# The rounded part of ten convolution weights: a casting transfer from GpSimd in place of ScalarE's copy

## The chip, the cores and the metric

The kernel runs on one core of one Trainium2 chip. The metric is the device time of one execution in microseconds. The engines are named as the profile names them: PE (TensorE), with its weight loads as PEld; DVE (VectorE); ACT (ScalarE); POOL (GpSimd); SP (SyncE, which here only issues transfers). A transfer that SP issues is in the profile's queue "hardware_dynamic", one that GpSimd issues in "software_dynamic".

## What is computed

One layer of a diffusion backbone, for 128 context tokens and 512 latent tokens, with model width 1024. What matters here is the mixer: one input projection feeds grouped-query attention (8 query heads, 2 key heads) and, beside it, a short gated convolution.

```python
h = _rms(x, norm_mix) * (1 + sc1) + sh1
proj = h @ w_in
q, k, v, gb, gc, u = jnp.split(proj, ...)      # 512, 128, 128, 512, 512, 512 columns
attn = _block_attention(rope(rms(q)), concat(ctx_k, rope(rms(k))), concat(ctx_v, v))
y_conv = gb * _short_conv(gc * u, conv_w)      # three taps along the tokens
mix = concat(_rms(attn), _rms(y_conv)) @ w_out
x = x + g1 * mix                               # then a SwiGLU block of width 2816
```

All inputs are float32. The vectors sh1, sc1, g1 and so on come from a separate product with the weights w_ada.

## The kernel before

**Split products.** PE multiplies in a rounded format, float32r. To keep accuracy every operand is kept in two parts: a high part, which is the value rounded to float32r, and a low part, which is the value less the high part. A product is then three matmuls: high by high, high by low and low by high. The helper `split` (line 171) makes the two parts: ScalarE copies into a float32r tile (line 172), VectorE subtracts that from the source (line 173).

**Stages.** Until about 76 us the kernel loads x and the first modulation weights, normalises x, and multiplies for the queries; the order of all engines is written out by hand there (P1SEQ). From there to about 260 us attention and the convolution run together, and here the change lies. PE's order is written by hand in this stage as well (the string SEQ: S is scores, T transposes of the probabilities, O the product with the values, F1 one piece of filler). The order of the other engines in this stage is set by the framework's scheduler from priorities. Then come the output projection and the feed-forward block, again in a hand-written order.

**Filler.** The filler is the convolution's projection (`conv_steps`, line 723) and the rest of the modulation product (`ada_all`, line 770). There are twelve convolution weights of 512 KB, for gc, u and gb in each of four column blocks (the list CONV, line 264). Each is multiplied in two token halves of 320 by eight blocks of 128 rows by three matmuls, at lines 715 to 717. So each weight has 16 matmuls at line 715.

**The weight stream.** Weights come in one list (`plan`, line 208): four for the queries, two for keys and values, the twelve of the convolution with sixteen 1 MB pieces of w_ada between them, and four of w_out. `W(key)` (line 252) is called where PE needs a weight, and loads up to three entries ahead. `load` (line 212) takes a tile wf from a ring of three (WFB) and lets SP load the float32 weight into it. `load_split` (line 233) takes wh and wl from rings of four each (WHB) and calls `split`, with a lowered priority (SOW). A buffer of wh can only be written again when PE has done with the weight four places earlier; a buffer of wf when VectorE's subtraction has read it. SP's queue also carries the small es transfers of attention (lines 909 and 910) and the w_ada pieces; GpSimd's holds the power function of the norms (line 186), four small memsets for each block of the convolution (line 734), and accumulating transfers (lines 755, 921, 922).

The first eight weights of the list, the first two of the convolution among them, are loaded in the first stage and split there by `w_hi` and `w_lo` (lines 532 to 543), which do not pass through `load_split`.

**Attention's chain.** For each head `att_s` (line 844) takes scores from PE (line 850), their maximum on VectorE (856), a scaling on ScalarE (857), the exponent on ScalarE (860), a reciprocal on VectorE (862) and the normalisation on ScalarE or VectorE (864, 866). `att_t` transposes the probabilities on PE (877) and splits them (172 and 173, to ph and pl). `att_o` multiplies by the values (894). The scores have one PSUM tile (tag "s", one buffer), so the next scores wait for the exponent.

Of the kernel before, what the change touches and what calls it, by code (L numbers as in the profile page):

```python
# [12 lines left out]
ALU = mybir.AluOpType  # L13
# [87 lines left out]
SOW = -300  # L101
# [12 lines left out]
def build(ctx, tc, x_prompt, x_sample, cond, cache_k, cache_v, vectors, b_ada, q_norm, k_norm, w_mod, w_ada,  # L114
          w_q, w_kv, w_conv, w_out, w_gate_up, w_down, rope, x_turned, o_turned, o_k, o_v):
    nc = tc.nc
    act, dve, pool, pe, sp = nc.scalar, nc.vector, nc.gpsimd, nc.tensor, nc.sync
# [23 lines left out]
    def T(tag, shape, dt=F32, bufs=1):  # L141
        seq[0] += 1
        return pools[where.get(tag, "A")][1].tile(list(shape), dt, tag=tag, bufs=bufs, name=f"{tag}_{seq[0]}")
# [21 lines left out]
    def f32(ap):  # L165
        return ap.bitcast(F32)

    def early(n):
        return tc.high_priority(n)

    def split(hi, lo, src):
        act.activation(hi, src, AF.Copy)
        dve.tensor_tensor(lo, src, f32(hi), ALU.subtract)
# [38 lines left out]
    def load(e, later=False):  # L212
        key, src, ph, ring, gain, _ = e
        if ring == "op":
            e[5] = [T(x, (P, 8, P), F32R, WHB) for x in ("wh", "wl")]
            with early(SOP[0]):
                split(*e[5], order[place["gu"[key[2] == "A2"], key[1]]][5])
            return
        a, b = src.shape[1], src.shape[2]
        wf = T("aw", (P, a, b), F32, AWB) if ring == "a" else T("wf", (P, a, b), F32, WFB)  # L220
        sp.dma_start(wf, src)
        if ring in "af":
            e[5] = wf
            return
        if later:
            deferred.append((e, wf))
            return
        load_split(e, wf)
# [4 lines left out]
    def load_split(e, wf):  # L233
        key, src, ph, ring, gain, _ = e
        a, b = src.shape[1], src.shape[2]
        wh = T(ring + "h", (P, a, b), F32R, WHB)
        wl = T(ring + "l", (P, a, b), F32R, WHB)
        if gain is None:
            with early(SOW):
                split(wh, wl, wf)  # L240
        else:
            for i in range(a):
                g = vec[:, gain + i:gain + i + 1]
                act.activation(wh[:, i], wf[:, i], AF.Copy, scale=g)
                dve.scalar_tensor_tensor(wl[:, i], wf[:, i], g, f32(wh[:, i]), ALU.mult, ALU.subtract)
        e[5] = (wh, wl)
# [1343 lines left out]
```

## Time and profile before

| What | us |
|---|---|
| Median of 3 runs | 720.96 |
| Lowest and highest run | 719.54, 721.59 |
| The profiled execution, its own time | 720.04 |
| Span of that execution | 718.2 |
| PE busy | 708.6 |
| PE weight loads busy | 678.0 |
| VectorE busy | 539.8 |
| ScalarE busy | 425.1 |
| GpSimd busy | 70.9 |

The span is the time from the first to the last instruction that the profile shows; the execution's own time is 1.84 us longer. A busy time is the sum over an engine's instructions in that one execution. Matmuls overlap in the profile, so PE's idle time is more telling than its busy time. "Idle before" names the work whose end released an instruction, as far as the profile shows it.

### The profile page before, as it was taken

How to read it: one execution, taken by the hardware profiler on the slowest of the kernel's cores; microseconds unless marked ns; L12 is line 12 of the kernel's file. 1: busy time of each engine (PE TensorE's matmuls, PEld its weight loads, DVE VectorE, ACT ScalarE, POOL GpSimd, SP SyncE). 2: the span in 40 equal slices, each digit the busy share in tenths (PEclk: the TensorE clock that was granted, in tenths of full speed). 3: DMA queues.
4: the chain of work that ended last, by engine and by line, in shares of the span. 5: the costliest groups of instructions: out<-in, count | busy, mean ns of one | idle time of the engine just before them, and what ended most of it. 6: DMA issues, size and time to landing. Idle time of an engine off the chain costs nothing.

```text
span 718.2 us, 12650 instructions
## 1 busy us (share of the span) xinstructions
PE 708.6 (99%) x4950; PEld 678.0 (94%) x4950; DVE 539.8 (75%) x976; ACT 425.1 (59%) x801; POOL 70.9 (10%) x101
## 2 busy tenths in 40 slices
PE   8999999999999999999999999999999999999997
PEld 7679798989988999999999999999999999999997
DVE  5767977675766556779988966579789855788895
ACT  6566877676676435565565655556556555465553
POOL 2303201012010121300000011000000011000000
PEclk9999999999999999999999999999999999999999
DMA  8964254546444222831323267522222556322462
GB/s 356 338 217 181 69 188 159 165 155 174 140 117 157 86 76 59 268 109 50 98 65 101 74 151 133 131 81 89 89 89 89 125 129 128 112 67 81 140 207 103
DMA packets 33884, 95.97 MB, mean 134 GB/s; under 512 B 4288, under 2 KB 12608, under 8 KB 31776
## 3 DMA queue, kind: packets, MB, share of 16 engines
q1 hardware_dynamic: 29360, 88.09, 36.2%
q0 software_dynamic: 4176, 7.01, 7.1%
q8 instruction: 39, 0.64, 0.4%
q14 instruction: 21, 0.17, 0.1%
q10 hardware_dynamic: 288, 0.05, 0.0%
HBM read 81.77 MB, written 10.62 MB: 129 GB/s over the span
## 4 chain that ended last, share of the span: by engine, by line
PE 92%; DVE 3%; ACT 3%; DMA 1%; issue 1%; SPq 0%; POOL 0%; DVEq 0%; ACTq 0%; POOLq 0%
PE pf L176 22%; PE pf L177 22%; PE pf L178 22%; PE pc L715 3%; PE pc L716 3%; PE pc L717 3%; PE po L894 3%; PE ps L850 2%; PE pt L877 2%; PE pc L776 2%; PE ps L176 1%; PE ps L178 1%; DMA es<-t 1%; PE ps L177 1%; PE pc L375 1%; PE pc L516 1%
## 5 line engine op out<-in xcount | busy, mean ns | idle before, releaser
L1361 DVE TENSOR_TENSOR wl<-sx,wh 128x1024 fp32r<-128x1024 f32 (+1 forms) x64 | 76.0, 1187 | 45.8 <-ACT wh L1358 45.8
L176 PE MATMUL pf<-B,wh 128*128 128x320 f32 x288 | 88.8, 308 | 0.0
L178 PE MATMUL pf<-B,wl 128*128 128x320 f32 x288 | 88.6, 308 | 0.0
L177 PE MATMUL pf<-B,wh 128*128 128x320 f32 x288 | 88.6, 308 | 0.0
L178 PE MATMUL pf<-T,wl 128*128 128x320 f32 x280 | 86.2, 308 | 0.0
L176 PE MATMUL pf<-T,wh 128*128 128x320 f32 x280 | 86.1, 308 | 0.0
L177 PE MATMUL pf<-T,wh 128*128 128x320 f32 x280 | 86.1, 308 | 0.0
L1358 ACT ACTIVATE wh<-sx 128x1024 fp32r<-128x1024 f32 (+1 forms) x64 | 65.7, 1027 | 4.1 <-PE pf L177 3.3
L715 PE MATMUL pc<-hH,wh 128*128 128x320 f32 x192 | 61.9, 323 | 0.0
L717 PE MATMUL pc<-hH,wl 128*128 128x320 f32 x192 | 59.3, 309 | 0.0
L716 PE MATMUL pc<-hL,wh 128*128 128x320 f32 x192 | 59.2, 308 | 0.0
L177 PEld LDWEIGHTS pf<-B,wh 128*128 128x128 f32 x288 | 54.0, 187 | 0.0
L176 PEld LDWEIGHTS pf<-B,wh 128*128 128x128 f32 x288 | 54.0, 187 | 0.0
L178 PEld LDWEIGHTS pf<-B,wl 128*128 128x128 f32 x288 | 54.0, 187 | 0.0
L178 PEld LDWEIGHTS pf<-T,wl 128*128 128x128 f32 x280 | 52.5, 187 | 0.1
L176 PEld LDWEIGHTS pf<-T,wh 128*128 128x128 f32 x280 | 52.5, 187 | 0.0
L177 PEld LDWEIGHTS pf<-T,wh 128*128 128x128 f32 x280 | 52.5, 187 | 0.0
L178 PE MATMUL pf<-gT,wl 128*128 128x320 f32 x160 | 49.3, 308 | 0.0
L176 PE MATMUL pf<-gT,wh 128*128 128x320 f32 x160 | 49.3, 308 | 0.0
L177 PE MATMUL pf<-gT,wh 128*128 128x320 f32 x160 | 49.3, 308 | 0.0
L1358 ACT ACTIVATE wh<-wf 128x1024 fp32r<-128x1024 f32 (+3 forms) x48 | 42.6, 888 | 0.8 <-PE pf L177 0.7
L1482 POOL DMA_DIRECT2D xd<-cu x16 | 13.9, 868 | 285.2 <-DVE cu L1469 255.9
(352 smaller groups left out, 2022.1 us busy)
## 6 DMA issues: line engine op xcount, KB each, us to landing
wf<-in_w_gate_up_dram SPq DMA_DIRECT2D x44, 512.0 KB, 3.4
aw<-in_w_ada_dram SPq DMA_DIRECT2D x16, 1024.0 KB, 6.6
af<-in_w_mod_dram SPq DMA_DIRECT2D x16, 512.0 KB, 6.3
wf<-in_w_down_dram SPq DMA_DIRECT2D x16, 512.0 KB, 3.5
wf<-in_w_conv_dram SPq DMA_DIRECT2D x12, 512.0 KB, 3.8
xd<-cu POOLq DMA_DIRECT2D x16, 320.0 KB, 4.6
wf<-in_w_out_dram SPq DMA_DIRECT2D x8, 512.0 KB, 4.1
wf<-in_w_down_dram SPq DMA_DIRECT2D x8, 384.0 KB, 3.2
```

The costliest lines, as they stand in the source:

```text
L176: pe.matmul(out, lh, rh, start=start, stop=False, skip_group_check=more)
L177: pe.matmul(out, lh, rl, start=False, stop=False, skip_group_check=more)
L178: pe.matmul(out, ll, rh, start=False, stop=stop, skip_group_check=more)
L715: pe.matmul(acc, wh[:, k], hH[k][:, c0:c0 + n], start=(k == 0), stop=False)
L716: pe.matmul(acc, wh[:, k], hL[k][:, c0:c0 + n], start=False, stop=False)
L717: pe.matmul(acc, wl[:, k], hH[k][:, c0:c0 + n], start=False, stop=(k == KD - 1))
L776: pe.matmul(rp[CG * g:CG * (g + 1)], cp[:, k], w[:, g], start=(k == 0), stop=(k == KD - 1), skip_group_check=True)
L850: pe.matmul(s2[:, g, :320], q, kk[:, v, P + g * 320:P + (g + 1) * 320], start=(i == 0), stop=(i == 1))
L877: pe.transpose(tp[:, i, h], u[3][h][:, kt * P:(kt + 1) * P], ident)
L894: pe.matmul(ov, w, x[:, i].rearrange("p a q -> p (a q)"), start=(g == 0 and i == 0 and n == 0), stop=(last and i == len(kts) - 1 and n == 1))
L1358: act.activation(wt[x, name][0], src, AF.Copy)
L1361: dve.tensor_tensor(wl, src, f32(wh), ALU.subtract)
```

## The change

For the weights of the convolution that pass through `load_split`, the high part wh is no longer made by ScalarE from wf. GpSimd issues a second transfer from the same place in HBM, whose destination is the float32r tile, so that the transfer itself casts. VectorE's subtraction stays, with its lowered priority, and reads both tiles; the new transfer has the ordinary priority. The plain load into wf by SP stays. The weights of w_out keep the old way, and so do the first two of the convolution.

```diff
         wh = T(ring + "h", (P, a, b), F32R, WHB)
         wl = T(ring + "l", (P, a, b), F32R, WHB)
-        if gain is None:
+        if key[0] == "conv":
+            pool.dma_start(wh, src)
+            with early(SOW):
+                dve.tensor_tensor(wl, wf, f32(wh), ALU.subtract)
+        elif gain is None:
             with early(SOW):
                 split(wh, wl, wf)
         else:
```

## The prediction

> **What bounds the kernel now.** I read the busy time by stage first, because the change touches one stage only. The columns are the stretch and its length, then the busy time (and instructions) of PE, its weight loads, VectorE (DVE), ScalarE (ACT) and GpSimd (POOL), the granted clock, the DMA engines' share and GB/s.
>
> ```profile
> 76.00:190.00 114.00, 112.13 (x825) 101.75 (x824) 84.19 (x172) 82.56 (x175) 15.50 (x27) 1.00 0.48 151
> 190.00:262.00 72.00, 70.43 (x510) 64.31 (x510) 47.38 (x93) 41.49 (x85) 7.92 (x12) 1.00 0.40 126
> 262.00:718.20 456.20, 452.52 (x3090) 451.92 (x3088) 355.94 (x564) 253.42 (x451) 29.25 (x31) 1.00 0.39 110
> sum 718.20, PE 708.62 PEld 677.98 DVE 539.76 ACT 425.09 POOL 70.88; mean PE 177.16 PEld 169.49 DVE 134.94 ACT 106.27 POOL 17.72
> ```
>
> PE is busy 708.62 of 718.20 us at a granted clock of 1.00. Between 76 and 190 us, where the changed transfers will lie, it is idle 114.00 - 112.13 = 1.87 us; from 190 to 262 us another 1.57. No relief of another engine in the changed stage can win more than the first number, plus what it moves in the second. Then what PE waits for there (76 to 190 us; total, times, longest):
>
> ```profile
> PE ps L850 <- ACT pr L860: 1.2, 2, 0.6
> PE po L894 <- DVE pl L173: 0.3, 1, 0.3
> PE po L660 <- ACT t L966: 0.3, 1, 0.3
> ```
>
> All three are links of the attention chain (scores L850, maximum, exponent L860, split, L894). None is a convolution weight. So ScalarE's rounding of those weights is not on the path by itself; it can only stand in front of a link of that chain.
>
> **ScalarE's part that goes.** The view of the tile wh between 76 and 190 us groups the rows; "until" lines say what the engine sat idle for.
>
> ```profile
> L172 ACT ACTIVATE wh<-wf x10: 1042/1060/1073, 78.9 to 185.6; 128x1024 fp32r<-128x1024 f32 x10
> L173 DVE TENSOR_TENSOR wl<-wf,wh x10: 1209/1216/1227, 82.8 to 186.7; 128x1024 fp32r<-128x1024 f32 x10
> ...
>   PE pc L716: 0.8, 2
> ```
>
> Ten of the twelve convolution weights take this way (the first two are split in the stage before, at lines 536 and 543, and stay). Removed: 10 x 1.060 = 10.6 us of ScalarE, from 82.56 to about 72 of 114 us. Nearly all of it lies beside PE work. On the path it can be worth at most the waits above, 1.2 + 0.3 + 0.3 = 1.8 us. The two that ScalarE's exponent ended, 1.2 us, are the likely ones; the order of DVE and ScalarE is set anew by the scheduler, so I take half of them: -0.6 us. VectorE's ten subtractions of 1.216 us stay, at other places.
>
> **When a weight is split, and when it is needed.** One weight in time order: its load is one of two that SP issues from 84.04, then ScalarE's rounding, then the subtraction.
>
> ```profile
> 84.04 3.11 SPq L221 DMA_DIRECT2D wf<-in_w_conv_dram  x2
> ...
> 102.47 1.06 ACT L172 ACTIVATE wh<-wf 128x1024 fp32r<-128x1024 f32 x1 [0.47 <-PE pc L716]
> ...
> 103.94 1.22 DVE L173 TENSOR_TENSOR wl<-wf,wh 128x1024 fp32r<-128x1024 f32 x1
> ```
>
> The plain data is in SBUF long before; the rounding waits 0.47 us for PE, because wh has a ring of four buffers and the weight four earlier must be used up. Each weight takes 16 matmuls of line 715, so the count says which one it is (line 715 from 60 us up to 102.6, then the start of the sixth weight):
>
> ```profile
> L715 PE MATMUL pc<-hH,wh x32: 302/309/417, 69.0 to 102.0; 128*128 128x320 f32 x32
> 145.94 0.39 PE L715 MATMUL pc<-hH,wh 128*128 128x320 f32 x1
> ```
>
> The second weight's last matmul starts at 102.0, the sixth weight (the fourth of the ten) is rounded at 102.47 and subtracted by 105.16, and PE first needs it at 145.94: 40.8 us of room. The casting transfer has to wait for the same buffer, so it starts no earlier than the rounding did. A few us more from there to the subtraction cost PE nothing directly. They do move the release of wf, for which SP's next weight load waits in SP's queue, with the two es transfers (L909, L910) behind it; that load too is used some 40 us later, and es feeds sums that are read much later. I cost both at nothing; the cover is those 40 us.
>
> **Ten transfers on GpSimd.** Its transfer instructions in this stage, and the wait before each:
>
> ```profile
> 86.76 0.94 POOL L921 DMA_DIRECT2D osq<-osq  x1 [3.06 <-ACT osq L917]
> 92.52 0.88 POOL L922 DMA_DIRECT2D osq<-osq  x1 [4.82 <-DMA osq<-osq]
> ...
> 133.94 0.91 POOL L921 DMA_DIRECT2D osq<-osq  x1 [15.35 <-ACT osq L917]
> 141.76 0.86 POOL L922 DMA_DIRECT2D osq<-osq  x1 [6.91 <-DMA osq<-osq]
> ```
>
> Ten more at about 0.9 us make 9 us, 15.5 to 24.5 of 114: GpSimd stays idle for most of the stage. The new instruction waits at the head of its queue for PE's release, and behind it stand the powers of line 186 (the queries' and keys' norms), the memsets of line 734 and the osq sums. If its place in the queue is as good as the rounding's was, that wait is 0 to 0.5 us, and none of these results is the last that PE waits for: 0.
>
> Traffic: 10 x 0.524 MB more. No row shows a cast, so its price is bounded by the plain queue and the queue of accumulating transfers (packets, MB, share of 16 engines), and by the plain load of the same bytes (median us to landing):
>
> ```profile
> q1 hardware_dynamic: 29360, 88.09, 36.2%
> q0 software_dynamic: 4176, 7.01, 7.1%
> ...
> wf<-in_w_conv_dram SPq DMA_DIRECT2D x12, 512.0 KB, 3.8
> ```
>
> Plain: 0.362 x 718.2 / 88.09 = 2.95 us of all engines per MB, 1.55 us for one weight. Accumulating: 0.071 x 718.2 / 7.01 = 7.27, so 3.8 us. Ten weights add 15 to 38 us to 0.48 x 114 = 55 us in that stage; the engines do not fill. Nothing for bandwidth.
>
> **The landing, and VectorE in front of it.** This is the cost that can reach PE. Today the subtraction waits for ScalarE; then it waits for a transfer, on a queue executed in order, and behind it stand the maxima, reciprocals and splits of attention. How long GpSimd's transfers take from issue to landing (tile osq, 76 to 262 us, 64 and 128 KB):
>
> ```profile
> DMA to landing us min/median/max: 2.3/4.3/7.6
> ```
>
> It is the spread that matters: 3.3 us between median and worst, though the transfers are alike. The scheduler places the subtraction in VectorE's order for one assumed landing; what lands later holds VectorE. How it fared with the es transfers speaks for good places (VectorE's waits, 76 to 190 us):
>
> ```profile
> DVE of L915 <- DMA es<-t: 0.6, 1, 0.6
> ...
> DVE of L916 <- DMA es<-t: 0.4, 1, 0.4
> ```
>
> That is 1.0 us over 14 transfers, 0.07 each; but es is 64 KB from SP. How much holding PE bears shows where an exponent's end meets the next scores that need its PSUM tile:
>
> ```profile
> 104.47 0.89 ACT L860 ACTIVATE pr<-ps,nsr,rq 128x640 f32<-128x640 f32 x1
> ...
> 105.50 0.56 PE L850 MATMUL ps<-KA,qT 128*128 128x320 f32 x2
> ...
> 147.27 0.89 ACT L860 ACTIVATE pr<-ps,nsr,rq 128x640 f32<-128x640 f32 x1
> ...
> 149.12 0.46 PE L850 MATMUL ps<-KA,qT 128*128 128x320 f32 x2
> ```
>
> Room of 105.50 - 105.36 = 0.14 us in one place, 149.12 - 148.16 = 0.96 in the other. Bounds for one load: 0 (placed behind the landing) and 3.3 - 0.14 = 3.2 us; below nothing only through ScalarE, counted above. I take the middle of the landing spread: five of ten land later than placed, by half of 3.3, 1.65 us, less 0.96 of room (the larger, since PE shows only four waits in 114 us and so has room at most steps): 5 x 0.69 = 3.4 us.
>
> One rule of the Trainium skill speaks against the change more strongly. The row: VectorE scales probabilities twelve times in this stage.
>
> ```profile
> L866 DVE TENSOR_SCALAR pr<-pr,nsr x12: 542/552/555, 86.9 to 188.2; 128x640 f32<-128x640 f32 x12
> ```
>
> The page "SBUF — State Buffer" (section "A bandwidth-pool intuition that's wrong") states that a transfer issued by GpSimd took about 620 ns alone and about 3100 ns beside a VectorE copy that takes the port they share, since GpSimd cannot write its descriptors meanwhile. By that figure an estimate would be 2.5 us of lateness for each load and a sum of +15 us. The rows above bear it out only so far that GpSimd's instructions themselves stayed at 0.86 to 0.94 us with VectorE busy for 84.19 of 114 us, while the landings scattered.
>
> **Sum.** -0.6 (ScalarE) + 3.4 (VectorE held) = +2.8 us. On the profiled execution, 720.04 us (span 718.2), that is 722.8; the median of the runs is 0.92 higher, 720.96, so the forecast is 723.8.
>
> **Rivals.** (1) *The holds stay covered, no change.* The subtractions are placed behind the landings as those of es are: ten at 0.07 us make +0.7, less 0.6: 721.1. For it: the 40 us of room and es; against it: the spread of 2.3 to 7.6 us. (2) *Faster: ScalarE's relief is what counts.* Attention's exponents and splits come earlier by up to 1.06 us wherever a rounding stood before them; the 1.87 us of idle PE in the stage go, and some of the 1.57 behind it: 2.5 us, 718.5. It decides if VectorE is never held beyond the room, and if nearly all idle time there is ScalarE's; against it: only 1.2 us is put down to the exponent. (3) *Every load is late by the full spread*, or the port rule's way: GpSimd writes its descriptors only between VectorE's operations; 10 x (3.3 - 0.55, the mean of the two rooms) - 0.6 = +27, 748. For it: nothing but the worst landing; against it: the median. (4) *The transfer moves the bits and does not round.* Then the low part is zero, and all instructions and transfers remain: the time is that of the other cases. The page "DMA: Bandwidth & Descriptors" (section "SWDGE vs HWDGE vs iDMA") says that a float32r destination always casts, from GpSimd alone; no run here shows it yet.
>
> **How the numbers follow.** A measurement here tells about 0.3%, 2.16 us, from no change. Forecast with its worse forms, (3) among them at 0.05: 0.45. No change: 0.41. Faster by over 0.3% needs more than the stage's whole idle time: 0.14. The forecast's own range, from just past the bound to about 1 us held per load (10 - 0.6 = +9.4), is 723.1 to 730.4. For 8 in 10 I take 718.7 to 732: below lies half of (2), above it (3) and some more.
>
> **What would show it.** In the changed profile: ten GpSimd transfers to wh of about 0.9 us, ScalarE's rounding from wf down to the four of w_out in that stage and its busy time 10 us lower; waits of VectorE's wl for the transfer of wh, several of 1 to 3 us; behind them PE waits for exponents or splits, 76 to 190 us growing to about 117 and everything after 262 us unchanged. Wrong if VectorE never waits for wh (then rival 1 or 2, told apart by PE's idle time in the stage), if GpSimd's queue blocks a power that PE needs, or if PE waits for a weight itself.

## The result, and the profile after

The changed kernel takes 730.63 us in the median of 4 runs (730.12 to 731.31); the kernel before, measured beside it, 720.56 (719.54 to 721.59, 4 runs). The ratio is 1.0140, with a 95% interval of 1.0122 to 1.0159: slower by 10.1 us. The profiled execution took 730.12 us with a span of 728.4, 10.2 longer than before.

The busy time by stage of the changed kernel, with the columns of the first fence of the prediction:

```profile
76.00:190.00 114.00, 105.99 (x750) 94.49 (x749) 78.13 (x158) 68.11 (x152) 18.47 (x33) 0.97 0.58 185
190.00:262.00 72.00, 70.21 (x515) 64.06 (x515) 48.39 (x96) 43.65 (x92) 10.60 (x15) 1.00 0.42 130
262.00:728.40 466.40, 462.75 (x3160) 462.15 (x3158) 361.21 (x574) 257.57 (x456) 29.05 (x31) 1.00 0.39 109
```

Two things changed in the first row. PE's idle time went from 1.87 to 114.00 - 105.99 = 8.01 us, and the granted clock from 1.00 to 0.97. The second row's idle time is 1.79 us (1.57 before), the third's 3.65 (3.68 before). So the loss lies between 76 and 190 us: 6.1 us more of idle PE, 0.2 in the second stage, and 114 x 0.03 = 3.4 us of matmuls at a lower clock. These make 9.7 of the 10.2 us. That the third stage only moved is seen in the matmuls of line 715, which is line 719 now; first the kernel before, then the changed one, between 60 and 262 us:

```profile
L715 PE MATMUL pc<-hH,wh x192: 302/309/417, 69.0 to 241.5; 128*128 128x320 f32 x192
```

```profile
L719 PE MATMUL pc<-hH,wh x192: 302/309/615, 68.9 to 251.7; 128*128 128x320 f32 x192
```

The convolution starts at the same time and its last matmul starts 10.2 us later. The median is still 309 ns, but the longest went from 417 to 615.

What VectorE waits for in the changed kernel, 70 to 265 us (total, times, longest); the two rows are those that end with a transfer:

```profile
DVE wl L241 <- DMA wh<-in_w_conv_dram: 10.8, 6, 4.2
DVE of L919 <- DMA es<-t: 5.6, 4, 3.3
```

Six of the ten subtractions stood at the head of VectorE's queue before their transfer had landed, for 1.8 us in the mean. The es sums, which waited 2.8 us in the same stretch before, are held 5.6 us. PE's waits in the same stretch:

```profile
PE ps L854 <- ACT pr L864: 2.5, 3, 1.4
PE pt L664 <- DVE KB L173: 1.7, 1, 1.7
PE po L898 <- DVE pl L173: 1.6, 2, 1.0
PE pt L664 <- DVE pl L173: 1.3, 1, 1.3
...
PE pt L881 <- ACT pr L868: 1.1, 1, 1.1
```

Not one of them is a wait for a weight. Those shown are links of attention, and the larger ones come right behind a held subtraction or a held es sum on VectorE. The two rows left out, of 1.1 and 0.2 us, stand in the kernel before as well; the 1.1 us are a wait for the convolution's sum ysum.

The transfers themselves, from the view of the tile wh (duration of an issue in ns, first and last start; the waits of each engine; the landing):

```profile
L239 POOL DMA_DIRECT2D wh<-in_w_conv_dram x10: 530/569/612, 74.3 to 195.1; - x10
L241 DVE TENSOR_TENSOR wl<-wf,wh x10: 1204/1226/1226, 78.2 to 201.0; 128x1024 fp32r<-128x1024 f32 x10
L172 ACT ACTIVATE wh<-wf x4: 1046/1054/1061, 210.5 to 252.2; 128x1024 fp32r<-128x1024 f32 x4
...
DMA to landing us min/median/max: 3.7/4.3/5.0
```

The landings scatter by only 1.3 us around 4.3. What scatters is the place of the subtraction: the last of the six stood at its place 4.19 us before the landing, almost as early as the transfer was issued.

The worst place is the first. VectorE from 78 to 84 us, before and after (start, duration, operation, and in brackets the wait):

```profile
78.23 0.68 DVE L173 TENSOR_TENSOR pl<-pt,ph 128x512 fp32r<-128x512 f32 x1
...
81.04 0.76 DVE L173 TENSOR_TENSOR KB<-pt,KA 128x256 fp32r<-128x256 f32 x2
...
82.80 1.21 DVE L173 TENSOR_TENSOR wl<-wf,wh 128x1024 fp32r<-128x1024 f32 x1
```

```profile
78.17 1.23 DVE L241 TENSOR_TENSOR wl<-wf,wh 128x1024 fp32r<-128x1024 f32 x1 [0.95 <-DMA wh<-in_w_conv_dram]
79.31 0.68 DVE L173 TENSOR_TENSOR pl<-pt,ph 128x512 fp32r<-128x512 f32 x1
...
81.71 0.76 DVE L173 TENSOR_TENSOR KB<-pt,KA 128x256 fp32r<-128x256 f32 x2
```

Before, the subtraction came behind the splits pl and KB; now it comes ahead of them, waits 0.95 us and works 1.23. PE at the same place in the changed kernel:

```profile
78.45 0.31 PE L721 MATMUL pc<-hH,wl 128*128 128x320 f32 x1
80.05 0.44 PE L664 MATMUL pt<-ident,mA 128*128 128x128 f32 x2 [1.29 <-DVE pl L173]
82.19 0.69 PE L664 MATMUL pt<-ident,mA 128*128 128x128 f32 x2 [1.70 <-DVE KB L173]
...
83.80 0.47 PE L720 MATMUL pc<-hL,wh 128*128 128x320 f32 x1
84.06 0.47 PE L721 MATMUL pc<-hH,wl 128*128 128x320 f32 x1
```

PE's order is fixed, so it stands still for 1.29 + 1.70 = 2.99 us. And then the matmuls start 0.26 us apart instead of 0.15 (78.31 to 78.45 before the stop). The granted clock says the same; three stretches of the changed kernel:

```profile
75.00:82.00 7.00, 4.15 (x29) 3.03 (x27) 5.63 (x17) 4.63 (x15) 1.27 (x2) 0.96 0.84 241
82.00:88.50 6.50, 6.31 (x24) 6.08 (x25) 4.12 (x10) 1.93 (x5) 1.89 (x5) 0.52 0.33 90
88.50:95.00 6.50, 6.39 (x46) 4.50 (x45) 4.24 (x8) 3.92 (x10) 1.52 (x2) 1.00 0.39 108
```

From 82 to 88.5 us the clock is at half; PE does 24 matmuls there and 46 in the 6.5 us behind it. A row of PE "busy for 6.31 of 6.50" hides this; the clock's column shows it.

### The profile page after: what moved, and what is told of

Same layout as the page of the kernel before. It is cut to its first block, busy times and chain, and to the rows that moved or that the text cites. A ratio compares the mean times of both kernels' runs of the same rounds, so it can differ in the third digit from the quotient of the medians.

```text
span 728.4 us, 12659 instructions
## 1 busy us (share of the span) xinstructions
PE 712.4 (98%) x4950; PEld 680.6 (93%) x4950; DVE 540.1 (74%) x976; ACT 417.1 (57%) x791; POOL 77.2 (11%) x111
## 4 chain that ended last, share of the span: by engine, by line
PE 85%; DVE 5%; ACT 4%; DMA 3%; issue 2%; POOL 0%; DVEq 0%; ACTq 0%; POOLq 0%
PE pf L176 21%; PE pf L178 21%; PE pf L177 21%; PE pc L719 2%; PE pc L720 2%; PE pc L721 2%; PE po L898 2%; DMA wh<-in_w_conv_dram 2%; DMA es<-t 2%; PE pt L881 2%; PE ps L854 1%; PE pc L780 1%; ACT pr L864 1%; PE ps L176 1%; PE ps L178 1%
```

## The experiments

The theory after this look: VectorE is held by subtractions placed ahead of their transfers, and PE stops where attention has no room (A). The rival: the added traffic delays the other transfers and GpSimd's queue, whatever VectorE does (B). The diffs are against the changed kernel, but those of experiments 1 and 5 are against the kernel before. The kernel before, measured beside the experiments, had medians of 719.40 (experiments 1 to 4), 719.98 (5 to 8) and 719.44 us (9).

**1. Traffic alone.** ScalarE's rounding is back, and the ten casting transfers go into a spare tile that nothing multiplies. A copy of one column by ScalarE times each of them.

```diff
+                if key[0] == "conv":
+                    spare = room_k[:, 1536:2560].bitcast(F32R).rearrange("p (a b) -> p a b", a=a)
+                    act.activation(spare[:, 0, 0:1], f32(wh[:, 0, 0:1]), AF.Copy)
+            if key[0] == "conv":
+                pool.dma_start(spare, src)
```

> The kernel before, and beside it the ten casting transfers, each issued by GpSimd behind ScalarE's rounding into a spare tile that nothing reads (ten one-column copies on ScalarE set their times). Theory A (VectorE is held in front of a landing that comes later than its place in the order, and one long hold halves PE's clock): no one waits for these transfers, so 720.6, at most 722. Rival B (the ten transfers themselves cost: GpSimd's queue, the DMA engines, other transfers slowed): the loss is there without any wait for wh, 728 to 731.

Measured: 730.51 us, ratio 1.0159 (1.0142 to 1.0176). By its number that is B, but the waits (ScalarE's and PE's, 70 to 265 us) show a hold that the experiment itself made:

```profile
ACT mA L243 <- DMA mA<-in_w_conv_dram: 6.8, 2, 4.9
```

```profile
PE ps L855 <- ACT pr L865: 6.6, 3, 5.5
```

The one-column copy writes the spare tile, so it has to wait for the transfer before it. It held ScalarE for 6.8 us in two places, the exponent behind it came late, and PE waited 5.5 us at once. The end of the convolution's second weight was 8.3 us later than before; from there to the twelfth weight nothing was added, though seven more transfers ran. That speaks against B, but the time as a whole doesn't tell A from B. It does show once more what an engine costs that is held in front of a landing, here ScalarE.

**2. The subtraction behind the second next maximum.** The changed kernel, with each subtraction put into VectorE's order by hand, behind the second maximum of a score after the transfer.

```diff
             pool.dma_start(wh, src)
-            with early(SOW):
-                dve.tensor_tensor(wl, wf, f32(wh), ALU.subtract)
+            late_subs.append([1, wl, wf, wh])
...
```

> The changed kernel, with each subtraction of the ten put behind a later score maximum in VectorE's order, so that the transfer has landed long before VectorE comes to it. Theory A: no wait of wl for wh, clock 1.00, PE idle from 76 to 190 us back near 2 us, 720 to 722. Rival B: the transfers are all there, 728 to 731.

Measured: 728.08 us, ratio 1.0116 (1.0100 to 1.0131): a miss for A's number, and within B's. But no subtraction waited for a transfer any more, and up to the eighth weight the loss was 1.9 us where the changed kernel has 10.0. Of the rest, 3.8 us came at the last weight, from the place chosen: nine subtractions came 21 to 39 us after the issue of their transfer, and the tenth, whose transfer was issued at 186.94 us, 48 us after it. PE then did wait for this one, and half clock followed (VectorE's row and PE's; then two stretches with the clock):

```profile
235.18 1.22 DVE L261 TENSOR_TENSOR wl<-wf,wh 128x1024 fp32r<-128x1024 f32 x1
```

```profile
236.45 0.41 PE L732 MATMUL pc<-hH,wl 128*128 128x320 f32 x1 [1.99 <-DVE wl L261]
```

```profile
230.00:240.00 10.00, 8.01 (x54) 6.29 (x54) 7.22 (x13) 5.98 (x12) 1.13 (x1) 0.89 0.33 99
240.00:262.00 22.00, 20.89 (x139) 20.57 (x138) 13.07 (x26) 10.03 (x18) 3.08 (x3) 0.89 0.19 54
```

The place can be too late as well as too early. The cover of "those 40 us" from a split to its use is not free to spend: the tenth subtraction used it up. A tile wf is free only when its subtraction has read it, so loads came late too (the last of the convolution was issued at 185.91 us, at 147.33 before); no row shows PE waiting for one of those.

**3. All but the first two.** The first two of the ten weights keep ScalarE's rounding.

```diff
-        if key[0] == "conv":
+        if key[0] == "conv" and key[1:] not in ((O_GB, 0), (O_GC, 1)):
```

> The changed kernel, but the first two of the ten weights go back to ScalarE; eight transfers are left. Theory A: the hold at 77 us and the stretch at half clock behind it go, about 5.5 of the 10 us: 724 to 726, clock 1.00. Rival B, a cost spread over ten transfers: 8/10 of 10 us, 728 to 729.

Measured: 724.86 us, ratio 1.0074 (1.0059 to 1.0089), within A. Stage and waits of this kernel:

```profile
76.00:190.00 114.00, 109.22 (x797) 98.08 (x797) 80.74 (x166) 72.72 (x160) 19.90 (x34) 1.00 0.55 182
```

```profile
DVE wl L241 <- DMA wh<-in_w_conv_dram: 9.0, 5, 3.7
DVE of L919 <- DMA es<-t: 5.1, 4, 2.9
```

VectorE is held nearly as long as in the changed kernel, 9.0 of 10.8 us, but the clock of this stage stays at 1.00 and PE's idle time is 4.78 us instead of 8.01. (Behind the wait for ysum, 3.41 us at half clock follow from 250.3 us; the profiled execution of the changed kernel has none there.) The two first transfers, with 0.95 and 1.32 us of holds, carry about half of the loss.

**4. The first one only.**

```diff
-        if key[0] == "conv":
+        if key == ("conv", O_GB, 0):
```

> Only the first of the ten weights comes from a casting transfer. Theory A: its hold of about 1 us and the subtraction behind it at 77 us keep PE idle for about 3 us, the clock halves for some us: 724 to 727, and nothing further. Rival B: a tenth of 10 us, 721 to 722.

Measured: 722.91 us, ratio 1.0050 (1.0033 to 1.0068): 3.5 us more than before, by one transfer of ten. Both numbers were missed, A's by 1.1 us and B's by 0.9. Told as a rise over the 720.56 us of the result above, A had foreseen 3.4 to 6.4 us and B 0.4 to 1.4; so the rise agrees with A, at its lower end. VectorE waits 0.8 us for it, PE 2.7, and the stage's clock is 0.99; the two rows of PE:

```profile
PE pt L664 <- DVE KB L173: 1.6, 1, 1.6
...
PE pt L664 <- DVE pl L173: 1.1, 1, 1.1
```

**5. Traffic alone, mended.** As 1, but GpSimd itself times the transfer, with a copy of one column out of wh into a tile of its own, so that no other engine waits.

```diff
+            if key[0] == "conv":
+                gate = pool.tensor_copy(T("gate", (P, 1)), f32(wh[:, 0, 0:1]))
+                with tc.issue_after(gate.ins):
+                    pool.dma_start(room_k[:, 1536:2560].bitcast(F32R).rearrange("p (a b) -> p a b", a=a), src)
```

> The control of the first traffic run, mended: the kernel before, with the ten casting transfers into a spare tile that nothing reads, now timed by a one-column copy on GpSimd that waits for ScalarE's rounding, so that neither ScalarE nor VectorE waits for a landing of these ten. VectorE's order is that of before. Theory A (only engines held by a late landing cost time): within 1 us of before, 719 to 721; VectorE may still be held by es transfers that land later beside them, up to 2 us of PE. Rival B (the ten transfers cost by themselves): 728 to 731.

Measured: 721.91 us, ratio 1.0030 (1.0015 to 1.0045). All ten transfers run (196 GB/s in the stage, more than the 185 of the changed kernel), and PE loses nothing there. The two rows are the changed stage and the one behind it:

```profile
76.00:190.00 114.00, 112.06 (x824) 101.80 (x825) 84.24 (x172) 82.37 (x174) 27.01 (x47) 1.00 0.60 196
190.00:262.00 72.00, 70.13 (x495) 63.62 (x493) 46.27 (x90) 40.11 (x82) 7.93 (x12) 0.98 0.40 125
```

PE's idle time in the changed stage is 1.94 us, 1.87 before. B is refuted: the traffic and GpSimd's queue cost 1 to 3 us by the interval, not 10. A's "within 1 us" is missed as well, by about 1 us. In the profiled execution the last matmul of the convolution starts only 0.6 us later than before; behind it follow 3.41 us at half clock (0.98 in the second row), which cost 1.7. The es sums do wait for their transfers here (5.2 us in six places, 2.8 before), and that is hidden for the most part.

**6. Each subtraction at a place behind its landing.** The changed kernel with a list: behind which maximum each of the ten is issued.

```diff
...
+            n = SUB_AT[CONV.index(key[1:])]
...
+    SUB_AT = {2: 1, 3: 3, 4: 4, 5: 7, 6: 10, 7: 13, 8: 16, 9: 19, 10: 21, 11: 24}
...
```

> The changed kernel, each of the ten subtractions put behind one named score maximum some 6 to 10 us after the release of its buffer: late enough for the landing, early enough that the ring of wf is not late for the weights of w_out, as it was in the first such run. Theory A: no wait of wl for wh, no half clock from 76 to 190 us; what is left is VectorE held by es (9.4 us in the first such run), worth about 2 us of PE: 721 to 723. Rival B: 728 to 731.

Measured: 724.15 us, ratio 1.0067 (1.0043 to 1.0092); the nine executions lie between 722.93 and 728.55. Five to six of the ten us are gone (5.3 by the ratios, 5.9 by the medians), with the same transfers, the same bytes and the same subtractions, which came 8 to 20 us after the issue; no subtraction waits for a transfer, and the clock is 1.00:

```profile
76.00:190.00 114.00, 110.10 (x803) 98.74 (x803) 81.06 (x167) 71.93 (x161) 19.99 (x36) 1.00 0.59 191
```

That is A's mechanism. Its number is a miss by some 1 us: 4.2 us of loss stay, 2.0 of them as idle PE in this row. VectorE still waits 7.0 us for es, once for 2.9.

**7. GpSimd rounds.** No second transfer at all: `pool.dma_start(wh, src)` becomes `pool.tensor_copy(wh, wf)`.

> The ten high parts are rounded by a copy on GpSimd from wf, with no second transfer; ScalarE is relieved as in the changed kernel. Theory A: VectorE waits for GpSimd's copy only as far as the copy lasts longer than its place in the order allows; with a copy of 2 to 4 us some holds of under 1 us: 719 to 723. Rival C (the new order of ScalarE and VectorE costs by itself, whatever makes the high part): 724 or more without a wait of wl for wh.

Measured: 723.03 us, ratio 1.0032 (1.0017 to 1.0048). ScalarE is relieved as in the changed kernel (72.67 us in the stage, 82.56 before), without a byte more, and nothing is won. The time lies at the upper end of A's range; C asked for no wait for the rounding, and there are two. VectorE's waits for the rounding (70 to 265 us):

```profile
DVE wl L241 <- POOL wh L239: 3.2, 2, 2.2
```

The first subtraction again stands in front of attention: it waits 1.0 us and then takes 2.08 us, beside GpSimd's copies, where the others take 1.21 to 1.23. PE waits 1.7 us behind it. So such a stop needs no transfer: a subtraction held at that place is enough.

**8. The es sums put later too.** Experiment 6, and every pair of es sums behind the second maximum after its transfers.

```diff
...
         sp.dma_start(esw[64:128], e[0:64, :, 1, :])
+        held.append([1, lambda: att_sum(t, v, e, esw)])
...
```

> As the run with the placed subtractions, and the sums that read es are put behind the second score maximum after them, too. Theory A: VectorE waits for no transfer any more, PE idle from 76 to 190 us at or below the 1.9 us of before: 718.5 to 720.5. Rival B: 728 to 731. If es alone explains nothing, the same time as with the subtractions placed.

Measured: 729.49 us, ratio 1.0129 (1.0103 to 1.0155): a miss for A, and within B's number, though the traffic is that of experiment 6. The sums were now so late that PE waited for what follows them, the accumulating transfers of osq (second row), and 3.41 us at half clock followed from 192.8 us:

```profile
PE po L917 <- DVE pl L173: 2.6, 4, 1.0
PE pt L1000 <- DMA osq<-osq: 2.5, 1, 2.5
```

**9. The es sums behind the next maximum.** One number of 8 changed, `held.append([0, ...`.

> The kernel with all subtractions placed behind the landing, in which the ten pairs of es sums are now queued behind the next maximum of a score, not the second next. Before that edit it measured 724.15 with 6.7 us of VectorE waiting for es from 70 to 265 us; with the second next maximum 729.49. Theory A: what was left of the loss (4.2 us over the kernel before) was VectorE held by es, and the second next maximum was only too late. Then the es waits fall to under 1 us, no transfer of osq is waited for by PE, and the time is 720 to 722.5. Theory B: the hold on es was covered, and the rest comes from the new order of VectorE and of the buffers' release as a whole. Then the es waits fall but the time stays at 723.5 to 726, or rises towards 729 as with the later place.

Measured: 723.09 us, ratio 1.0057 (1.0037 to 1.0077), which can't be told from experiment 6. PE no longer waits for osq. The es waits fell from 7.0 us to 4.2 (the expectation has 6.7 for the 7.0), and one pair of es sums still found its transfer 3.0 us away, so neither theory got its condition. How much of the last 4 us is es and how much the new order of VectorE stays open.

No version came out faster than the kernel before.

## Why the prediction was right or wrong, point by point

The sign was right, and so was the mechanism in the main, VectorE held in front of a landing; the size was not: +2.8 us on the profiled execution were forecast and +10.1 came.

**The step that failed** is the term "VectorE held 3.4". It had three parts. How late: "five of ten", by 1.65 us, 8.3 in all; there were six, 10.8 in all. This was close, but by luck: I put the lateness down to the scatter of the landings, and they lie within 3.7 to 5.0 us. The subtraction's place is what varies. I had also taken the transfer to start no earlier than the rounding did (78.9 us before); the first was issued at 74.30, and its subtraction moved from 82.80 ahead to 78.17. Experiment 6 moved the places alone and took the waits away. How much is covered: "less 0.96 of room" at every hold. This was wrong in kind. Room is a property of the place, and not of the mean hold: the first hold, 0.95 us, had none and was followed by 2.99 us of idle PE in two waits, since the subtraction's own 1.23 us stood ahead of the splits too; the holds of 1.47 us at 130 us and 2.09 us at 173 us were followed by no wait of PE, and that of 4.19 us at 185 us by 0.95 us. The prediction had found a place with 0.14 us of room and took the larger value for all. What a stop of PE costs: I counted one us for one us. The first stop was followed by 6.8 us at half clock, 3.4 us more, for which the sum had no term. Experiments 3 and 4 show these two effects of the first transfers together: without the first two, 4.8 us less by the ratios (0.0066 of 720.56); the first alone, 3.5.

**"I cost both at nothing"** (SP's next load and the es transfers) failed in the second part. The first part held in the changed kernel: PE waits for no weight. But the es sums were read at once, not "much later". The worst case stands in SP's and VectorE's rows of the changed kernel, issue of the two transfers and the sum:

```profile
136.24 0.60 SPq L913 DMA_DIRECT2D es<-t  x1
136.89 0.60 SPq L914 DMA_DIRECT2D es<-t  x1
```

```profile
141.07 0.42 DVE L919 TENSOR_TENSOR of<-t,es 64x256 f32<-64x256 f32 x1 [3.33 <-DMA es<-t]
```

At 136.45 us GpSimd had issued a casting transfer of 512 KB. The sum waited 3.33 us, and at 143.16 PE waited 1.06 us for a normalised probability (the row `PE pt L881` above). That the casting transfer made this es late is likely by the order of the issues. In general the added traffic does it: from issue to landing the es transfers took 2.1 us in the median and 3.8 at most before, 2.4 and 4.8 in the changed kernel, 2.4 and 4.2 in experiment 5, which adds the traffic alone, and 2.1 and 3.2 in experiment 7, which adds none. What it costs is only bounded: es waits of 5.2 us cost at most 3 us in experiment 5.

**ScalarE, -0.6:** not seen. Its busy time fell from 425.1 to 417.1, by 8.0 us and not by 10, and PE's waits for the exponent rose from 1.5 to 2.5 us between 70 and 265 us. Experiment 7 relieves ScalarE without a transfer and wins nothing. The reading behind it held, that ScalarE's rounding was not on the path.

**GpSimd's queue, 0:** right. The ten issues took 0.57 us each, not 0.9; the powers behind them were not waited for by PE. Its long wait for a free buffer at the head of its queue (38.6 us in six places) cost PE nothing that a row shows.

**Bandwidth, nothing:** right to within the 1 to 3 us of experiment 5. From the profile's queues of the changed kernel, with those of before in the prediction,

```profile
q1 hardware_dynamic: 29360, 88.09, 35.4%
q0 software_dynamic: 5616, 12.26, 9.5%
...
wh<-in_w_conv_dram POOLq DMA_DIRECT2D x10, 512.0 KB, 4.3
```

the queue of GpSimd took 0.095 x 728.4 - 0.071 x 718.2 = 18.2 us of all engines more for 5.25 MB, 1.8 us for a weight, near the lower of the two bounds (1.55 and 3.8).

**The rule of the page "SBUF — State Buffer"** in the Trainium skill (section "A bandwidth-pool intuition that's wrong"), by which I had put 2.5 us of lateness on each load, speaks of a VectorE copy. VectorE's scaling of the probabilities ran beside, or right behind, the issue of only two of the ten, from 91.36 and 126.31 us; these two landed after 4.3 and 5.0 us, at most 0.7 behind the median of 4.3. So the lengthening by 2.5 us was not seen, and the other eight don't test it. The sum of +15 by that rule is nearer to the result than mine, but not by its mechanism.

**The rivals.** (1), holds covered, would have needed VectorE not to wait for transfers; it waits 16 us in all, 2.8 before. (2), faster, needed the same. (3), every load late by the full spread, has the right mechanism and too high a count: 6 holds instead of 10, most of them with some room. (4) can't be told from the times. **What would show it:** the rounding of ScalarE down to four, the ten GpSimd transfers, PE's waits for exponents and splits, and the unchanged part behind 262 us were found as written. VectorE's waits lie between 0.7 and 2.1 us, with one of 4.2, where 1 to 3 was written; the 76 to 190 us of work grew by about 9.5 us, not 3.

## What to carry to other kernels

Before an operation that waited for a neighbouring engine is made to wait for a transfer, look at what stands behind it in its own engine's order: price each hold at its place, by the room of the chain behind it, and not by the mean landing. Where the order comes from a scheduler, look up in the first profile whether the consumer was placed ahead of the landing (its waits for the transfer) and place it by hand, neither ahead of the landing nor so late that the user of its result, or the next load into its source buffer, waits for it. And a stop of PE of some 3 us in a stage that is otherwise full is to be priced with the time at half clock behind it.

## What the runs showed of the hardware

The half clock. In the trace's record of the granted clock every such stretch inside these kernels, apart from the last 2 us of the span, lasts 3.41 us or twice that: 6.83 us in the changed kernel, 3.41 in experiments 1 to 5, 8 and 9 (two stretches in 2). Matmuls of 128x320 start 0.26 us apart in it instead of 0.15. At half speed 3.41 us cost 1.7.

The page "TensorE: Matmul & The Clock Gate" of the Trainium skill (section "What's actually happening") states a free-running window of 3413 ns and two settings only, half and full; the records agree with the length and the settings. Its section "Why this matters for your kernels" advises against idle gaps of more than about 3 us. Here shorter ones were followed by half clock: in the changed kernel the drop came at 81.5 us, 1.0 us into the second of two gaps of 1.29 and 1.70 us with 0.4 us of transposes between them. And the wait of 1.1 us for ysum near 250 us, which every version has, is followed by 3.41 us at half clock in the profiles of experiments 2, 3, 5 and 9 and not in those of the other versions; so the same gap sometimes costs 1.7 us more and sometimes not. That fits a window which doesn't start with the kernel; no run here isolates it.

A transfer that casts 512 KB to float32r took 3.7 to 5.0 us from issue to landing (median 4.3), and the plain load of the same bytes from SP 3.9 in the median in the same execution. How much of the 0.4 us is the cast and how much the other queue was not separated.
